# An expert stage with other weight rows, other sums and a fixed order on TensorE

## The chip, the core and the metric

The kernel runs on one core of one Trainium2 chip. Every time is in microseconds (us) of device time for one execution of the whole program. The core has a matrix engine (TensorE, in the profile PE for its products and PEld for its weight loads), a vector engine (VectorE, DVE), a scalar engine (ScalarE, ACT), GpSimd (POOL) and SyncE (SP), which here only issues DMAs. Each engine works through its own list of instructions in order and waits on semaphores for the others. Products are summed in eight PSUM banks of 128 partitions by 512 fp32 numbers.

## What is computed

Two transformer blocks over 256 tokens of width 1024. The first block (two layers, each with a feed-forward net, a token mix of four branches, a gated per-layer input and a second feed-forward net) and the mixer of the second block come first. The change is about what comes last, a mixture of experts: 32 experts, each token goes to four of them.

```python
def moe_ffn(h, w_router, b_router, w1, b1, w2, b2):
    logits = xt @ w_router + b_router
    top_v, top_e = lax.top_k(logits, TOP_K)          # 4 of 32
    weights = jax.nn.softmax(top_v, axis=-1)
    ...
    hcat = x_pad[tok] @ w1[e] + b1[e]                # [tokens, 1024] @ [1024, 2048]
    x_glu = jnp.minimum(hcat[:, ::2], SWIGLU_LIMIT)
    x_lin = jnp.clip(hcat[:, 1::2], -SWIGLU_LIMIT, SWIGLU_LIMIT)
    act = x_glu * jax.nn.sigmoid(SWIGLU_ALPHA * x_glu) * (x_lin + 1.0)
    return act @ w2[e] + b2[e]                       # [tokens, 1024] @ [1024, 1024]
```

The output is `x + g_f * moe_ffn(h, ...)`, where `h` is a modulated RMS norm of `x`. All weights are fp32.

## The kernel before, in words

**The first block and the mixer.** Their weights come through SP into 512 KB buffers named `raw`. ScalarE rounds each to float32r (`whi`, L143), VectorE or GpSimd subtracts (`wlo`, L147), and TensorE makes three products of each (L205 to L207). Layer norms run on VectorE (L266 to L275), token tile 0 first, then tile 1. Beside all this a side job `ada` multiplies the conditioning vector with a 1024 by 6144 matrix: 96 loads `araw` of 256 KB each on SP (L813), two buffers, and 96 sums `acc` on VectorE (L822). A list scheduler sets where those stand among the other instructions.

**The expert stage.** Experts go in 16 pairs, e and e+1, with room for 64 tokens each. For a pair, SP loads 24 weight units of 1 MB (L1440, tile `mraw`, and one buffer `AS`) into a ring of 18 buffers, in the order of their use: 16 for the up product, 8 for the down product. A unit is 256 rows by 1024 columns of one expert; row 128k+p lies on partition p, so each partition receives two runs of 4 KB. In the last pair the down units are 512 rows by 512 columns, in runs of 2 KB.

On TensorE one expert of the pair uses the left 64 columns of the array and the other the right 64. One up or down step is a product of 128x64 by 128x512 for each expert, and the two run side by side. The parts of a pair are: `moe_gather` (L1350, one-hot matrix `S` from L1338 times the tokens gives `xe`), `moe_bias` (L1379, a selector times the table `b1`, opens the banks), `moe_up` (L1389) for the first 1024 columns, then for the second, each followed by the activation (L1399 to L1403, with a tanh on ScalarE at L1400), `moe_aT` (L1409, transposes, copied by ScalarE at L1410), `moe_back` (L1363, the weighted return matrix `wT`), `moe_down` (L1423, scaled at L1427 into `ys`) and `combine` (L1471, `ys` times `wT`). `combine` adds the 16 pairs up in four banks over the whole stage; x is added at the very end (L1528) and stored (L1529). The gather and the bias of the next pair are given to the scheduler in the middle of the pair's second up product (`ahead`, L1512), so that their instructions stand among its steps.

Of the kernel before, what the change touches and what calls it, by code (L numbers as in the profile page):

```python
# [31 lines left out]
def constants():  # L32
    """Tables that depend on shapes alone."""
# [33 lines left out]
def arow(ap, n, parts=P):  # L67
    """A row of n numbers in DRAM, read by every partition."""
    return bass.AP(tensor=ap.tensor, offset=ap.offset, ap=[[0, parts], [1, n]])


class Kernel:
# [15 lines left out]
    # ---------------------------------------------------------------- helpers  # L88
# [31 lines left out]
    def rsqrt(self, v, eps, n, scale=1.0):  # L120
        """1/sqrt(v*scale+eps) by Newton steps on VectorE."""
# [19 lines left out]
    def split_from(self, src, hi, lo, pool=False):  # L141
        """hi = src rounded to float32r, lo = src - hi, both exact parts."""
# [36 lines left out]
    def gemms(self, lhs, nk, w, parts):  # L179
        """Several column ranges (first, width, done, onpool, granules) of one weight, tile 0 of all first."""  # L180
# [12 lines left out]
    def products(self, lhs, nk, width, banks, t, grans):  # L193
        """What the granules add to the banks of tile t."""
# [14 lines left out]
    def load_split(self, nk, w, c0, width, xn=0, onpool=()):  # L209
        """The granules of a weight: (first row chunk, number of chunks, hi, lo)."""  # L210
# [18 lines left out]
    def trans4(self, srcs, ident=None):  # L229
        """Up to four [128, <=128] pieces, transposed into one bank."""  # L230
# [5 lines left out]
    def to_T(self, src, t, xh, xl, c0, n):  # L236
        """chunks c0..c0+n of the natural tile src -> split, transposed tiles."""
# [12 lines left out]
    # --------------------------------------------------------------- layernorm  # L250
# [7 lines left out]
    def layer_norm(self, t, banks, coef, gb, last=False):  # L258
        """x[t] <- LN(coef*banks + x[t]); the new x^T; x[t] scaled for the next residual."""
# [33 lines left out]
    # -------------------------------------------------------------------- FFN  # L293
# [63 lines left out]
    def consts(self):  # L357
        """What comes beside the first product: the second tile of x, tables and constants."""
# [10 lines left out]
    def tables(self):  # L369
        """cos and sin of positions * inv_freq, [128, 2 tiles, 48]."""  # L370
# [34 lines left out]
    def gelu2(self, x, out, tmp):  # L405
        """out = 2*gelu(x) (tanh form)."""
# [7 lines left out]
    def proj(self, mp, lhs, w, c0, width, onpool=()):  # L414
        """natural [128, 2, width] of x @ w[:, c0:c0+width]."""
# [4 lines left out]
    def projs(self, mp, lhs, w, *parts):  # L420
        """Several of them, tile 0 of all first; a part is first column, width, onpool, granules."""
# [12 lines left out]
    def softmax_rows(self, S, n, keys, scale=1.0, extra=None):  # L434
        """In place exp(scale*(S - rowmax)) of S [128, n, keys]; returns 1/sum [128, n]."""
# [236 lines left out]
    def merge(self, mp, lhs, w_in, g0, wb, yTs, order, nk, then=None):  # L672
        """sum over n of 2*sigmoid(gate_n) * (y_n @ w_branch_n), natural [128, 1024] per tile."""
# [77 lines left out]
    def ple(self, L):  # L751
        """x[t] += sigmoid(x @ w_ple_gate) * (p @ w_ple); the second product fills the wait for the first."""
# [22 lines left out]
    # ----------------------------------------------------------- second block  # L775
# [14 lines left out]
    def ada(self, r0, r1):  # L790
        """Half rows r0.. of silu(c) @ w_ada + b_ada, into DRAM, in steps beside other work; 1 + both scales."""
# [42 lines left out]
    def mod_row(self, dst, i, norm=None):  # L834
        """dst [128, 1024] <- row i on every partition; with norm: row * norm."""
# [8 lines left out]
    def mod_pair(self, pool, i, norm):  # L844
        """The factor and the shift of a modulated norm."""
# [5 lines left out]
    def rms_mod(self, t, h, A, sh, split=True):  # L851
        """h <- x[t] * rsqrt(mean square) * A + sh, and its transpose, split or not."""
# [8 lines left out]
        xT = self.new_xT(t)  # L861
        for c in range(2):
            s = slice(c * 512, c * 512 + 512)
            nc.vector.scalar_tensor_tensor(h[:, s], x[:, s], r[:, 0:1], A[:, s], op0=OP.mult, op1=OP.mult)
            nc.vector.tensor_tensor(h[:, s], h[:, s], sh[:, s], op=OP.add)
# [8 lines left out]
    def lru_consts(self):  # L874
        """softplus(-lambda) times -2 and -4 per channel; half gate biases; conv weights."""
# [43 lines left out]
    def lru(self, mp, xr, gr, yT):  # L919
        """RG-LRU on [128 channels, 4, 256 tokens] tiles; writes its split output."""  # L920
# [25 lines left out]
        # with a = exp(L), u = tanh(L / 2): sqrt(1 - a^2) = sqrt(-u) * (1 + a)  # L946
# [22 lines left out]
    def rel_rows(self, mp):  # L969
        """Per head the bias row over query-key distance 255..-127, in DRAM; masked distances -1e30."""  # L970
# [13 lines left out]
        # one copy per partition, so that a pitch of one less skews the rows against each other  # L984
# [743 lines left out]
```

## Time and profile before

| what | value |
|---|---|
| time, median of 3 runs | 2582.32 us (2578.15 to 2583.32) |
| the profiled execution, span | 2582.4 us |
| TensorE busy | 2477.6 us, 96% of the span |
| VectorE, ScalarE, GpSimd busy | 1220.3, 815.1, 225.2 us |
| expert stage, first up step to the end | 1594 to 2582 us |
| share of 16 DMA engines in the expert stage | 102% (1700 to 2500 us) |
| HBM traffic | 704 MB read; 403 MB of it expert weights |

The profiled execution took as long as the median of the runs, so the sums of the prediction are made against its span. The span's first 60% belong to the first block and the mixer, the rest to the 16 pairs. The share of DMA time can pass 100% by a little, since transfers overlap at their edges. A matmul of fp32 leaves two records in the trace, so a step shows as two.

### The profile page before, as it was taken

To read this page: it belongs to the slowest core of one execution; us is meant where nothing else is said; L and a number is where in the kernel's file an instruction comes from. 1 tells how busy PE (TensorE), PEld (TensorE's weight loads), DVE (VectorE), ACT (ScalarE), POOL (GpSimd) and SP (SyncE) were. 2 spreads that over 40 slices of the span, in tenths; PEclk is the share of its full clock that TensorE was granted. 3 is DMA by queue.
4 is the path that set the end of the run, shared out by engine and by line. 5 is a ranking of instruction groups with operands and counts; after the bars stand their busy time and mean duration, and the time that the engine had idled before them with its cause. 6 is when DMAs were issued, how large, how long until landed. Compare 5 with 4: busy or idle time off the path is not lost.

```text
span 2582.4 us, 29195 instructions
## 1 busy us (share of the span) xinstructions
PE 2477.6 (96%) x11140; PEld 1611.5 (62%) x11140; DVE 1220.3 (47%) x2059; ACT 815.1 (32%) x1159; POOL 225.2 (9%) x197
## 2 busy tenths in 40 slices
PE   8999999999799999999988999999999999999998
PEld 6888787778678878778867776333333333333333
DVE  6767757776666775755567863111111111111111
ACT  5444544444344454444435641000000000000000
POOL 4000121200200011220031020000000000000000
PEclk9999999999899999999999998999999999999999
DMA  8775566667566646655655578999999999999995
GB/s 262 242 236 168 160 193 198 221 223 237 176 216 206 198 140 189 197 191 184 196 183 157 160 245 297 402 398 407 401 409 408 408 403 408 407 408 405 408 406 202
DMA packets 252697, 707.23 MB, mean 274 GB/s; under 512 B 18042, under 2 KB 31562, under 8 KB 252552
## 3 DMA queue, kind: packets, MB, share of 16 engines
q1 hardware_dynamic: 245032, 684.02, 73.9%
q0 software_dynamic: 7520, 21.29, 2.7%
q8 instruction: 90, 1.47, 0.2%
q14 instruction: 55, 0.45, 0.1%
HBM read 704.13 MB, written 3.47 MB: 274 GB/s over the span
## 4 chain that ended last, share of the span: by engine, by line
PE 77%; DVE 10%; DMA 5%; issue 4%; ACT 2%; POOL 1%; SPq 0%; DVEq 0%; ACTq 0%; POOLq 0%
PE sc L1389 19%; PE mm L206 12%; PE mm L207 12%; PE mm L205 12%; PE tp L1423 9%; PE tp L233 3%; PE tp L1350 2%; PE mm L1471 2%; DVE wlo L147 2%; DMA araw<-in_w_ada_dram 2%; PE sc L1379 1%; DMA raw<-in_ffn_up_dram 1%; ACT whi L143 1%; PE tp L1409 1%; DMA raw<-in_w_in_dram 1%
## 5 line engine op out<-in xcount | busy, mean ns | idle before, releaser
L147 DVE TENSOR_TENSOR wlo<-raw,whi 128x1024 fp32r<-128x1024 f32 (+1 forms) x459 | 568.8, 1246 | 292.4 <-ACT whi L143 289.9
L143 ACT ACTIVATE whi<-raw 128x1024 fp32r<-128x1024 f32 x486 | 509.6, 1055 | 538.2 <-PE mm L207 386.8
L206 PE MATMUL mm<-wlo,xTh 128*128 128x512 f32 (+2 forms) x1552 | 593.8, 383 | 9.5 <-POOL wlo L147 8.3
L205 PE MATMUL mm<-whi,xTh 128*128 128x512 f32 (+2 forms) x1552 | 599.6, 387 | 3.4 <-ACT whi L143 3.4
L207 PE MATMUL mm<-whi,xTl 128*128 128x512 f32 (+2 forms) x1552 | 594.0, 383 | 0.4 <-DVE xTl L147 0.4
L1389 PE MATMUL sc<-mraw,xe 128*64 128x512 f32 x1904 | 494.8, 598 | 0.0
L206 PEld LDWEIGHTS mm<-wlo,xTh 128*128 128x128 f32 x1552 | 295.4, 190 | 67.8 <-POOL wlo L147 11.3
L205 PEld LDWEIGHTS mm<-whi,xTh 128*128 128x128 f32 x1552 | 295.5, 191 | 61.0 <-ACT whi L143 5.9
L207 PEld LDWEIGHTS mm<-whi,xTl 128*128 128x128 f32 x1552 | 295.5, 190 | 52.4 <-DVE xTl L147 0.8
L1389 PEld LDWEIGHTS sc<-mraw,xe 128*64 128x64 f32 x1904 | 166.7, 136 | 254.0 <-issue 247.1
L1400 ACT ACTIVATE mt<-act 128x256 f32<-128x256 f32 x64 | 26.7, 417 | 720.8 <-DVE act L1399 708.6
L1423 PE MATMUL tp<-mraw,xTl 128*64 128x512 f32 x936 | 235.2, 595 | 9.8 <-ACT xTl L1410 9.6
L1399 DVE TENSOR_SCALAR act<-sc 128x256 f32<-128x256 f32 x62 | 26.3, 424 | 362.7 <-PE sc L1389 359.5
L1423 PEld LDWEIGHTS tp<-mraw,xTl 128*64 128x64 f32 x936 | 72.9, 137 | 148.7 <-issue 135.0
L1427 DVE TENSOR_TENSOR xTh<-tp,gf 128x512 f32<-128x512 f32 x32 | 22.1, 691 | 245.6 <-PE tp L1423 245.6
L207 PE MATMUL mm<-whi,hl 128*128 128x512 f32 x352 | 138.0, 392 | 0.0
L205 PE MATMUL mm<-whi,hh 128*128 128x512 f32 x352 | 137.8, 391 | 0.0
L206 PE MATMUL mm<-wlo,hh 128*128 128x512 f32 x352 | 137.6, 391 | 0.0
L822 DVE SCALAR_TENSOR_TENSOR acc<-araw,cond,acc 128x512 f32<-128x512 f32 x96 | 75.7, 788 | 50.2 <-DMA araw<-in_w_ada_dram 49.6
L147 POOL TENSOR_TENSOR wlo<-raw,whi 128x1024 fp32r<-128x1024 f32 x27 | 69.6, 2593 | 280.9 <-ACT whi L143 277.0
L694 POOL TENSOR_TENSOR pj<-pj,gt 128x512 f32<-128x512 f32 x32 | 58.1, 1827 | 239.3 <-DVE gt L693 238.1
L206 PEld LDWEIGHTS mm<-wlo,hh 128*128 128x128 f32 x352 | 66.4, 189 | 13.4
(423 smaller groups left out, 2178.4 us busy)
## 6 DMA issues: line engine op xcount, KB each, us to landing
mraw<-in_w_dram SPq DMA_DIRECT2D x362, 1024.0 KB, 16.2
raw<-in_ffn_up_dram SPq DMA_DIRECT2D x176, 512.0 KB, 4.4
raw<-in_w_in_dram SPq DMA_DIRECT2D x142, 512.0 KB, 4.2
raw<-in_ffn_down_dram SPq DMA_DIRECT2D x88, 512.0 KB, 4.3
araw<-in_w_ada_dram SPq DMA_DIRECT2D x96, 256.0 KB, 3.8
AS<-in_w_dram SPq DMA_DIRECT2D x21, 1024.0 KB, 14.8
raw<-in_w_branch_dram SPq DMA_DIRECT2D x28, 512.0 KB, 3.8
raw<-in_w_out_dram SPq DMA_DIRECT2D x24, 512.0 KB, 4.6
```

What stands on the lines that cost most here:

```text
L143: ins = self.nc.scalar.activation(hi, src, AF.Copy)
L147: ins = (self.nc.gpsimd if pool else self.nc.vector).tensor_tensor(lo, src, hi, op=OP.subtract)
L205: nc.tensor.matmul(banks[b], xh, hi[:, s], start=kc == 0, stop=False)
L206: nc.tensor.matmul(banks[b], xh, lo[:, s], start=False, stop=False)
L207: nc.tensor.matmul(banks[b], xl, hi[:, s], start=False, stop=kc == nk - 1)
L233: self.nc.tensor.transpose(pt[:s.shape[-1], i * P:i * P + s.shape[0]], s, self.ident)
L694: nc.gpsimd.tensor_tensor(m, m, th, op=OP.add)
L822: nc.vector.scalar_tensor_tensor(acc, raw, self.cond[:, k:k + 1], acc, op0=OP.mult, op1=OP.add)
L1350: nc.tensor.matmul(pg[c // 4][:, c % 4 * P:c % 4 * P + P], self.h2[t][:, c * P:c * P + P], S[:, t], start=t == 0 and c % 4 == 0, stop=t == ...
L1389: self.upped = nc.tensor.matmul(ph[nb][e * 64:e * 64 + 64], xe[:, k, e * 64:e * 64 + 64], u[:, (k % 2) * D + nb * 512:(k % 2) * D + nb * 5 ...
L1423: nc.tensor.matmul(py[c][e * 64:e * 64 + 64], aT[:, k * P + e * 64:k * P + e * 64 + 64], u[:, :512], start=k == 0, stop=k == 7)
L1471: self.nc.tensor.matmul(out[t][c], w[:, t, :], ys[:, c * 512:c * 512 + 512], start=start, stop=stop)
```

## The change

- **Weight rows.** Row 8p+k lies on partition p. A unit is one such k for the up product (2048 columns) or two for the down product (2 times 1024 columns): each partition receives one run of 8 KB. From partition to partition the addresses step by 64 KB in the up weights and by 32 KB in the down weights. The last pair's down product loads its first four k like the others and the last four by column halves, in runs of 2 KB. What meets the weights is permuted to match: `rms_mod` reads x and its two factors at a step of eight numbers for the expert norm (L864, L865 of before), the router's rows are loaded as 8p+k, and the last operation of the activation writes in another order.
- **The up product** runs over all 2048 columns at once in four banks: for k below 6 all four banks for each k, then k = 6 and 7 bank by bank. The activation follows for four banks.
- **Sums into x.** Every pair's `combine` goes into banks of its own and VectorE adds the result to x, one pair later.
- **Biases** are multiplied in float32r: the table is split into a high and a low part in 128 rows, two tables for 32 experts, so a selector of 512 columns and four products remain.
- **TensorE in program order.** All products of the stage pass through `pe`, which forbids the scheduler to move them.
- The DMA scratch of the program is set to 8192 bytes, which also moves where tiles lie.

```diff
     def route_prep(self, mp):
-        nc.gpsimd.dma_start(wr, a["w_router_2"][0].rearrange("(k p) n -> p k n", p=P))
+        nc.gpsimd.dma_start(wr, a["w_router_2"][0].rearrange("(p k) n -> p k n", k=KD))
...
+        for i in range(2):
+            raw = self.st(self.wp, [P, 1024], "raw", bufs=self.nraw)[:, :512]
+            hl = self.st(mp, [P, 512], f"b1{i}", F32R)
+            for h in range(2):
+                nc.gpsimd.dma_start(raw[64 * h:64 * h + 64], src[64 * i:64 * i + 64])
+            self.pin(nc.scalar.activation(hl, raw, AF.Copy))
+            self.pin(nc.vector.tensor_tensor(hl[64:], raw[64:], hl[64:], op=OP.subtract))
...
+    def pe(self, ins):
+
+        self.pin(ins)
+        return ins
...
     def moe_up(self, mp, xe, ph, units):
...
+        cut = KD - 2
+        steps = [(k, nb) for k in range(cut) for nb in range(4)] + [(k, nb) for nb in range(4) for k in range(cut, KD)]
+        for k, nb in steps:
+            for e in range(2):
+                self.pe(nc.tensor.matmul(ph[nb][e * 64:e * 64 + 64], xe[:, k, e * 64:e * 64 + 64],
+                                         units[e][k][:, nb * 512:nb * 512 + 512], start=False, stop=k == KD - 1))
...
-            nc.vector.scalar_tensor_tensor(g, l, 1.0, g, op0=OP.add, op1=OP.mult)
+            o = act.rearrange("s (k p) -> s p k", k=KD)[:, 32 * nb:32 * nb + 32]
+            nc.vector.scalar_tensor_tensor(o, l.rearrange("s (p k) -> s p k", k=KD), 1.0,
+                                           g.rearrange("s (p k) -> s p k", k=KD), op0=OP.add, op1=OP.mult)
...
     def sources(self, e):
-                return w[e + d, r, c].rearrange("(k p) n -> p k n", p=P)
-            return w[bass.ds(e[d], 1), r, c].rearrange("o (k p) n -> p (o k) n", p=P)
-        up = [rows(W1, d, j, q * D) for q in range(2) for j in range(4) for d in range(2)]
...
+                v = w[e + d].rearrange("(p k) n -> p (k n)", k=KD)
+            else:
+                v = w[bass.ds(e[d], 1)].rearrange("o (p k) n -> p (o k n)", k=KD)
+            return v[:, j * n:j * n + n]
+        up = [rows(W1, d, j, 2 * D) for j in range(8) for d in range(2)]
...
+    def combine(self, ys, w, cs=(0, 1), out=False):
+        for c in cs:
+            s = slice(c * 512, c * 512 + 512)
             for t in range(2):
-                self.nc.tensor.matmul(out[t][c], w[:, t, :], ys[:, c * 512:c * 512 + 512], start=start, stop=stop)
+                po = self.ps("tp")
+                self.pe(nc.tensor.matmul(po, w[:, t, :], ys[:, s], start=True, stop=True))
+                nc.vector.tensor_tensor(self.x[t][:, s], self.x[t][:, s], po, op=OP.add)
...
     def moe(self, mp):
         for e in range(0, NE, 2):
...
+            act = self.moe_up(mp, xe, ph, u1)
+            if end:
+                self.combine(*done)
+            else:
+                xe = self.moe_gather(mp, self.pos[:, :, e + 2:e + 4])
+            wT = self.moe_back(mp, self.pos[:, :, e:e + 2], self.Wh[:, :, e:e + 2])
+            self.moe_aT(act, aT)
+            self.moe_down(aT, ys, u2, (lambda: self.combine(ys, wT, (0,), True)) if end else None)
...
+            if done:
+                self.combine(*done)
...
+            done = ys, wT
+            ph = bias(e + 2)
...
-    nc = _bacc.Bacc("TRN2", target_bir_lowering=False, num_devices=1)
+    nc = _bacc.Bacc("TRN2", target_bir_lowering=False, num_devices=1, dynamic_dma_scratch_size=8192)
```

TensorE before, in the second half of a pair's up product: the rows L1389 are up steps of this pair, L1350 the gather of the next one, L1363 the return matrix.

```order
L1389 MATMUL sc_16242<-mraw_16162,xe_16077 64x512
L1363 MATMUL tp_16302<-ident,Sw_16298 128x128
L1350 MATMUL tp_16317<-S_16313,h_13106 128x128 x4
L1350 MATMUL tp_16318<-S_16313,h_13106 128x128 x2
L1389 MATMUL sc_16241<-mraw_16164,xe_16077 64x512
L1389 MATMUL sc_16242<-mraw_16164,xe_16077 64x512
L1350 MATMUL tp_16318<-S_16313,h_13106 128x128 x2
L1350 MATMUL tp_16317<-S_16313,h_13107 128x128 x4
L1389 MATMUL sc_16241<-mraw_16166,xe_16077 64x512
L1389 MATMUL sc_16242<-mraw_16166,xe_16077 64x512
```

TensorE now, at the end of a pair's up product (L1417 its last steps, L1369 the gather of the next pair, L1382 the return matrix, L1439 the transposes of the activation, L1456 the first down step).

```order
L1417 MATMUL mm_16768<-mraw_16801,xe_16671 64x512
L1417 MATMUL mm_16768<-mraw_16803,xe_16671 64x512
L1369 MATMUL sc_16922<-S_16918,h_13118 128x128 x4
L1369 MATMUL sc_16923<-S_16918,h_13118 128x128 x4
L1369 MATMUL sc_16922<-S_16918,h_13119 128x128 x4
L1369 MATMUL sc_16923<-S_16918,h_13119 128x128 x4
L1382 MATMUL tp_16946<-ident,Sw_16942 128x128 x2
L1439 MATMUL tp_16952<-ident,act_16885 128x128 x4
L1439 MATMUL tp_16958<-ident,act_16885 128x128 x4
L1456 MATMUL sc_16965<-mraw_16805,xTl_3743_16951 64x512
```

The gather stood between up steps, and up steps of one expert came two in a row; now it stands in one piece behind the last step, and the steps of the two experts alternate.

VectorE before, in the layer norm that closes the first feed-forward net of layer 0 (x_71 is token tile 0, mm the banks).

```order
L266 SCALAR_TENSOR_TENSOR x_71<-mm_1527,x_71 128x512
L267 BN_STATS bn_353_1747<-x_71 128x6
L266 SCALAR_TENSOR_TENSOR x_71<-mm_1528,x_71 128x512
L267 BN_STATS bn_353_1747<-x_71 128x6
L269 BN_AGGR mv_354_1752<-bn_353_1747 128x2
```

VectorE now, at the same place.

```order
L266 SCALAR_TENSOR_TENSOR x_71<-mm_1527,x_71 128x512
L267 BN_STATS bn_353_1747<-x_71 128x6
L822 SCALAR_TENSOR_TENSOR acc_4070<-araw_4073,cond,acc_4070 128x512
L822 SCALAR_TENSOR_TENSOR acc_4070<-araw_4075,cond,acc_4070 128x512
L266 SCALAR_TENSOR_TENSOR x_71<-mm_1528,x_71 128x512
L822 SCALAR_TENSOR_TENSOR acc_4070<-araw_4090,cond,acc_4070 128x512
L267 BN_STATS bn_353_1747<-x_71 128x6
L822 SCALAR_TENSOR_TENSOR acc_4070<-araw_4099,cond,acc_4070 128x512
L269 BN_AGGR mv_354_1752<-bn_353_1747 128x2
```

Sixteen sums of the side job, which stood in the second feed-forward net of layer 0, now stand in this layer norm and the start of the token mix behind it.

SP at the same place, the difference of the two lists (raw_1942 and its neighbours are weights of the token mix).

```order
 L219 DMA raw_1942<-in_w_in_dram 128x2x512
+L808 DMA acc_4070<-in_b_ada_dram 1x512
+L813 DMA araw_4073<-in_w_ada_dram 128x512
+L813 DMA araw_4075<-in_w_ada_dram 128x512
+L808 DMA acc_4267<-in_b_ada_dram 1x512
+L813 DMA araw_4090<-in_w_ada_dram 128x512
+L813 DMA araw_4099<-in_w_ada_dram 128x512
+L813 DMA araw_4116<-in_w_ada_dram 128x512
+L813 DMA araw_4125<-in_w_ada_dram 128x512
 L219 DMA raw_1948<-in_w_in_dram 128x2x512
```

The loads of the side job stand ahead of weight loads of the token mix; with two buffers `araw`, each waits until VectorE has used the one before the last.

## Rows read from the trace of the kernel before

**Rows 1.** The head of the page.
```profile
span 2582.4 us, 29195 instructions
```
**Rows 2.** Busy time by stretch; the last three: granted clock, DMA share, GB/s.
```profile
1595.00:1600.00 5.00, 5.00 (x26) 1.57 (x24) 0.00 (x0) 0.00 (x0) 0.00 (x0) 1.00 0.19 33
...
1700.00:2500.00 800.00, 785.08 (x3239) 304.19 (x3236) 121.93 (x309) 53.20 (x116) 0.00 (x0) 1.00 1.02 406
2056.00:2058.00 2.00, 2.00 (x12) 1.17 (x12) 0.15 (x1) 0.00 (x0) 0.00 (x0) 1.00 1.03 410
...
2540.00:2542.00 2.00, 2.00 (x10) 0.74 (x7) 0.00 (x0) 0.00 (x0) 0.00 (x0) 1.00 1.05 390
...
2546.00:2549.00 3.00, 3.00 (x16) 1.26 (x14) 0.00 (x0) 0.00 (x0) 0.00 (x0) 1.00 0.73 274
```
**Rows 3.** Waits of SP's queue, 1620 to 2582: total us, times, longest.
```profile
SPq L1440 <- PE sc L1389: 377.3, 136, 9.4
SPq L1440 <- PE tp L1423: 207.0, 100, 9.6
```
**Rows 4.** The chain that ended last, one pair: start us, us, what.
```profile
1698.37 13.95 PE tp L1423 x62
1712.32 3.63 PE mm L1471 x8
1715.95 13.95 PE sc L1389 x64
...
1729.93 0.42 DVE act L1399
...
1731.20 0.44 PE tp L1409 x2
...
1739.01 1.34 PE tp L1350 x12
...
1759.60 0.61 ACT xTl L1410
...
1760.25 4.93 PE tp L1423 x21
```
**Rows 5.** Groups by line and shape, 1700 to 2500 (13 pairs): count, busy, mean ns.
```profile
L1379 PE MATMUL sc<-b,sel 128*128 128x512 f32 x102 | 56.7, 637 | 2.1
```
**Rows 6.** The chain at the start of the expert stage.
```profile
1590.42 3.57 PE mm L1350 x16
1593.99 11.36 PE mm L1389 x49
```
**Rows 7.** Adding the shift in the expert norm, L865: ns min/median/max.
```profile
L865 DVE TENSOR_TENSOR h<-h,AS x4: 681/682/683, 1568.0 to 1581.5; 128x512 f32<-128x512 f32 x4
```
**Rows 8.** The chain at the end of the stage.
```profile
2574.70 2.00 PE mm L1471 x4
...
2576.73 0.69 DVE xTl L1528
```
**Rows 9.** Stretches at half clock, columns as in rows 2.
```profile
1588.10:1594.90 6.80, 6.52 (x28) 5.55 (x30) 3.08 (x19) 1.19 (x2) 0.00 (x0) 0.50 1.02 405
...
656.30:666.50 10.20, 3.05 (x12) 2.71 (x13) 8.64 (x23) 1.25 (x3) 0.00 (x0) 0.50 0.56 177
...
536.80:540.20 3.40, 3.40 (x12) 2.65 (x11) 3.30 (x6) 0.60 (x1) 0.00 (x0) 0.50 0.54 177
```
**Rows 10.** The chain in two layer norms, at 200 us and at 645 us.
```profile
200.28 0.70 DVE x L266
...
209.76 0.63 PE tp L233 x4
...
646.91 5.58 DMA araw<-in_w_ada_dram
...
663.45 1.08 PE tp L233 x4
...
667.12 0.23 PE mm L205
```

More of the change, by code (lines that the diff above doesn't have):

```diff
@@ new lines, in moe_up, with moe_aT @@
+            nc.vector.scalar_tensor_tensor(o, l.rearrange("s (p k) -> s p k", k=KD), 1.0,
+                                           g.rearrange("s (p k) -> s p k", k=KD), op0=OP.add, op1=OP.mult)
+        return act
+    def moe_aT(self, act, aT):
+        for q in range(2):
+            pt = self.ps("tp")
+            for j in range(4):
+                c = slice((q * 4 + j) * P, (q * 4 + j) * P + P)
+                self.pe(self.nc.tensor.transpose(pt[:, j * P:j * P + P], act[:, c], self.ident))
+            self.nc.scalar.activation(aT[:, q * 512:q * 512 + 512], pt, AF.Copy)
@@ new lines, in moe_down, with step, scale @@
+    def moe_down(self, aT, ys, units, last=None):
+        nc = self.nc
+        py = [self.ps("sc") for _ in range(2)]
+        def step(k, c):
+            for e in range(2):
+                if last and k >= 4:
+                    w = units[e][2 + c][:, k % 4 * 512:k % 4 * 512 + 512]
+                else:
+                    w = units[e][k // 2][:, k % 2 * D + c * 512:k % 2 * D + c * 512 + 512]
+                self.pe(nc.tensor.matmul(py[c][e * 64:e * 64 + 64], aT[:, k * P + e * 64:k * P + e * 64 + 64], w,
+                                         start=k == 0, stop=k == 7))
+        def scale(c):
+            s = slice(c * 512, c * 512 + 512)
+            nc.vector.tensor_tensor(ys[:, s], py[c], self.gf[:, s], op=OP.mult)
@@ L1417, in moe_down @@
         steps = [(k, c) for k in range(KD) for c in range(2)]
         if last:
-            steps.sort(key=lambda kc: kc[1])
+            steps = steps[:8] + [(k, c) for c in range(2) for k in range(4, KD)]
         for k, c in steps:
-            for e in range(2):
-                u = units[e][2 * c + k // 4][:, k % 4 * 512:] if last else units[e][k // 2][:, k % 2 * D + c * 512:]
-                nc.tensor.matmul(py[c][e * 64:e * 64 + 64], aT[:, k * P + e * 64:k * P + e * 64 + 64], u[:, :512],
-                                 start=k == 0, stop=k == 7)
@@ L1425, in moe_down @@
-        for c in range(2):
-            s = slice(c * 512, c * 512 + 512)
-            nc.vector.tensor_tensor(ys[:, s], py[c], self.gf[:, s], op=OP.mult)
+            step(k, c)
+            if k == 7:
+                scale(c)
+            if last and (k, c) == (5, 1):
+                last()
     def mtile(self):
@@ L1519, in moe @@
-            acc = acc or [[self.ps("mm") for c in range(2)] for t in range(2)]
-            self.combine(ys, wT, acc, e == 0, e == NE - 2)
-            if e == 0:
-                self.bias2(mp, acc)
-                nov = nc.values_load(self.nov[0:1, 0:1], min_val=0, max_val=NOV - 1)
-        self.acc = [self.big(f"xT{h}0") for h in "hl"]
-        for c in range(2):
-            for t in range(2):
-                s = slice(c * 512, c * 512 + 512)
-                nc.vector.tensor_tensor(self.acc[t][:, s], self.x[t][:, s], acc[t][c], op=OP.add)
-                nc.sync.dma_start(self.out[0, t * P:t * P + P, s], self.acc[t][:, s])
+            end = e == NE - 2
@@ new lines, in moe @@
+            act = self.moe_up(mp, xe, ph, u1)
+            if end:
+                self.combine(*done)
+            else:
+                xe = self.moe_gather(mp, self.pos[:, :, e + 2:e + 4])
+            wT = self.moe_back(mp, self.pos[:, :, e:e + 2], self.Wh[:, :, e:e + 2])
+            aT = self.big(f"xTl{i}")
+            self.moe_aT(act, aT)
+            ys = self.big(f"xTh{i}")
+            self.moe_down(aT, ys, u2, (lambda: self.combine(ys, wT, (0,), True)) if end else None)
+            if end:
+                self.combine(ys, wT, (1,), True)
+                break
@@ L1538, in bias2 @@
         for t in range(2):
-            nc.tensor.transpose(pw[:NE, t * P:t * P + P], self.W[:, t], self.ident)
-        wT = self.st(mp, [P, 2, P], "wT")[:NE]
+            self.pe(nc.tensor.transpose(pw[:NE, t * P:t * P + P], self.W[:, t], self.ident))
+        wT = self.st(mp, [P, 2, P], "wT", bufs=2)[:NE]
         nc.scalar.activation(wT, pw[:NE, :256].rearrange("p (t q) -> p t q", t=2), AF.Copy)
-        for t in range(2):
-            for c in range(2):
-                nc.tensor.matmul(acc[t][c], wT[:, t, :], b2[:, c * 512:c * 512 + 512], start=False, stop=False)
+        self.combine(b2, wT)
     def overflow(self, mp, nov):
```

151 lines of the change are left out of this document (63 added, 88 removed).

## The prediction

> **What bounds the kernel now.** I read the table of stretches first. From 1700 to 2500 us TensorE is busy 785 of 800 us at full clock, and in the same stretch the DMA engines run at a share of 1.02 and move 406 GB/s [rows 2]. Both are full, so the next question is who waits for whom. The waits of SP's queue answer it: the weight loads wait 377.3 and 207.0 us for up and down steps to free a buffer [rows 3]. TensorE sets the pace and the DMA follows close behind. The chain of one pair gives the pace: the down products of two pairs start at 1698.37 and 1760.25, so a pair takes 61.9 us [rows 4]. A pair's weights are 24 x 1.0486 = 25.2 MB, which at 406 GB/s is 62.0 us and at the 410 of an undisturbed stretch 61.4 us [rows 2]. A change that only shortens TensorE's pair can therefore win next to nothing; one that only speeds up the loads neither. This one touches both, and the sum must be made for each.
>
> The start and the end tell how much of the DMA's time lies between. In 1595 to 1600 it moves 33 GB/s, because the ring is full until the first up steps have run, and the rate falls again in 2546 to 2549 [rows 2]. The 366 units after the first 18 are 383.8 MB; at 406 GB/s they take 945 us, and 1600 + 945 = 2545, which agrees. The remaining 37 us to the end of the span at 2582.4 [rows 1] are TensorE working off its backlog.
>
> **The loads, 8 KB runs.** Before has only 4 KB runs, and 2 KB runs in the last pair. With 16 engines, 390 GB/s at 2 KB is 32768/390 = 84.0 ns a run; 406 to 410 at 4 KB is 161.4 to 159.8 ns [rows 2]. Another 2 KB thus costs 77.4 to 75.8 ns and the fixed part is 7 to 8 ns. By the same line a run of 8 KB takes 316 to 311 ns, or 414 to 421 GB/s. I take 417: 383.8/0.417 = 920 us, 25 us less. No row shows 8 KB runs, so the bounds are wide: above, no fixed part at all, 131072/(4 x 75.8) = 432 GB/s and 888 us; below, the 390 GB/s of the slowest runs shown and 984 us. I stay near the line through the two rows, since they are the same queue, the same tensors and the same ring.
>
> The Trainium skill, "DMA: Bandwidth & Descriptors", section "Latency and other measured facts", speaks against the new addresses: copies whose partitions lie a large power of two apart ran at 207 GB/s for a step of 512 KB and 103 for 4 MB, against 214 otherwise. Here the step is 64 and 32 KB, smaller than any in that list, and no row of before shows such a step. By a loss of the first size (207/214) 417 would become 403 GB/s and the gain would be gone; it is the second rival below.
>
> **TensorE's pair.** Up: two halves of 13.95, 27.9 us. Down 13.95, combine 3.63 [rows 4]. The gather: 12 records take 1.34, so its 32 take 3.6; ten transposes as long as such a record 1.1 [rows 4]. The biases were 102 records and 56.7 us in 13 pairs, 4.4 a pair [rows 5]; four float32r products at 0.23 [rows 10] are 0.9. Idle: after the last up step the activation of the last bank must run (1729.93 to 1731.20, 1.3 us [rows 4]) and the one-hot matrix of the gather is queued behind it on VectorE, an estimated 1 us more; the copy of the transposes, 0.6 [rows 4]; the selector behind the sums into x, about 1.2 by one sum as long as the last addition [rows 8] and its own copy. Sum 55.2 us. What it saves against 61.9 lies in the second up product: the 28.4 us from 1731.20 to 1759.60 [rows 4] hold 13.95 of up steps beside transposes, gather, biases and the idle time of the activation, and steps of one expert in a row, which lose the overlap of the two experts. What the program order costs is cover: gather and transposes now have no up steps beside them. The clock may follow. The shortest stretch at half clock (0.50 of the full 2.4 GHz) that the rows show lasts 3.4 us, at 536.8 [rows 9], and costs half of that. With two of them, 1.7 us each, a pair is 58.6.
>
> A pair's loads at 417 GB/s are 60.4 us. So the loads bind, TensorE catches up in a few pairs, and then waits 2 to 5 us a pair, at the last two k of the up product. Four sums of 0.69 into x per pair and the strided write of the activation lie on VectorE, which has 122 us of work in 800 [rows 2]: free.
>
> **The start.** The whole gather of pair 0 now stands behind all routing. Half of it was done earlier; the half that was left took 3.57 us at half clock [rows 6, 9], so the up product starts 3.6 us later than 1593.99. The strided reads of the norm are not shown in before. The operations are 0.68 us each [rows 7] and four per tile lie on the path: between nothing and twice as long, 0 to 2.8 us. I take 1, since most of the path around them is TensorE's. The loads resume at 1600 + 4.6 = 1604.6.
>
> **The end.** Loads end at 1604.6 + 920.4, plus 0.7 for four units in 2 KB runs: 2525.7. The last up unit lands 8 units, 20.8 us, before that. From it: 7 of the 32 up steps 6.1, activation 1.3, the waiting combine 3.6, transposes 1.1, copy 0.6, down 13.95 with half a combine 1.8 inside, 28.5 us, which is 7.7 behind the last load. Then scale 0.7, combine 2.0 and addition 0.7 [rows 8], and the store: the last addition ended at 2577.4 and the span at 2582.4, 5.0. That is 16.1, where before had 37. End: 2541.8.
>
> **Layer 0.** The lists show a term that the edit does not name: 16 sums of the side job and their loads move from the second feed-forward net into the layer norm at 200 us. That norm takes 9.5 us before TensorE gets its transposes [rows 10]. The norm at 645 has sums between its instructions in the very order that the first one now gets; from its wait for the load (5.58 us) to the transposes it takes 16.5 us, 7 more, and TensorE comes out of it with 10.2 us at half clock, 5 more [rows 9, 10]. Token tile 1 follows with sums too, and weight loads of the token mix queue behind the side job's. So up to 20 us can be lost. Gains stand against this: the second feed-forward net loses those sums, its half-clock stretch at 537 among the possible savings [rows 9]. Bounds -4 and +20; I take +8, nearer the norm at 645 than nothing. Forecast 2541.8 + 8 = 2550.
>
> **Rivals.**
> 1. The loads get no faster with longer runs. Then 945 instead of 920 us and 2575. For it: 410 GB/s may be the limit of something else than runs. Against: 390 and 410 differ with the run alone.
> 2. The loads get slower: every partition's run lies 64 KB from the next, and what serves the addresses takes that badly. It decides from 403 GB/s on (953 us to the end at 2582); at 390, 2613. For it only the page; against it no row, since before has steps of 4 and 8 KB.
> 3. TensorE's order binds. If every idle moment costs a half-clock stretch as long as the 6.8 us of the routing [rows 9], a pair is 55.2 + 6.8 = 62.0. Then 1598.6 + 15 x 62.0 + 58.7 for the last pair and its end + 8 = 2595, slower. It decides from 61.1 a pair. For it: three idle moments per pair where before had covered ones. Against: the idle moments are shorter than those in the norms.
> 4. All of it works and layer 0 costs nothing: 421 GB/s and 2533, with the gain of 4 there 2529.
>
> **Chances.** Forecast (2535 to 2570) 0.57, rival 1 0.13, rival 2 0.10, rival 3 0.08, rival 4 0.12. A measurement of this kernel can tell about 0.2% from no change. Faster: 0.56 of the forecast, all of rival 4, 0.06 of rival 1: 0.74. Same: 0.01, 0.06 of rival 1 and 0.03 of rival 3: 0.10. Slower: rival 2, 0.05 of rival 3 and 0.01 of rival 1: 0.16. The range from 2520 to 2592 leaves out the worse half of rivals 2 and 3 and a rate above 428 GB/s.
>
> **What would show it.** Right: 415 to 420 GB/s between 1700 and 2500, SP's queue no longer waiting for up and down steps but up steps for loads, a pair of 60 us, and some 17 us between the last load and the end. The layer norm at 200 us shows sums and a gap of several us on TensorE. Wrong: a rate at or under 406 (rivals 1 and 2), or half clock in each pair with SP still waiting for TensorE (rival 3).

## The result, and the profile after

The changed kernel takes 2553.7 us, the median of four runs (2552.11 to 2555.68), against 2582.82 for the kernel before: a ratio of 0.990 (95%: 0.9883 to 0.9916), faster by about 1%. Its profiled execution has a span of 2550.5 us, where before had 2582.4 [rows 1]. All readings of after in this section are of that execution.

The head of the page of after, and the shares of the span on its chain of waits by engine:

```profile
span 2550.5 us, 29146 instructions
...
PE 40%; DMA 36%; DVE 7%; issue 2%; ACT 2%; POOL 1%; SPq 0%; DVEq 0%; ACTq 0%; POOLq 0%
```

DMA is 36% of the chain: over a third of the span ends on a transfer. The loads of expert weights, the tiles `mraw` and `AS`, are 31 of these 36 points.

Stretches of after (length, busy time of PE, PEld, DVE, ACT, POOL; then granted clock, DMA share, GB/s): the layer norm at 210, a gap in the mixer, the start of the expert stage with the ring still full, the bulk of the stage, and its last up steps.

```profile
209.60:216.50 6.90, 0.00 (x0) 0.00 (x0) 6.90 (x15) 0.00 (x0) 0.00 (x0) 0.67 0.94 271
...
1519.20:1526.00 6.80, 3.38 (x7) 2.27 (x8) 3.17 (x3) 3.69 (x4) 0.00 (x0) 0.50 0.92 327
...
1610.00:1615.00 5.00, 5.00 (x26) 1.68 (x24) 0.00 (x0) 0.00 (x0) 0.00 (x0) 1.00 0.21 51
1615.00:1620.00 5.00, 5.00 (x26) 1.61 (x24) 0.00 (x0) 0.00 (x0) 0.00 (x0) 1.00 1.00 418
...
1700.00:2450.00 750.00, 695.77 (x3118) 266.37 (x3114) 161.16 (x343) 50.69 (x108) 0.00 (x0) 0.98 1.01 421
...
2510.00:2516.00 6.00, 5.18 (x13) 1.49 (x14) 1.78 (x4) 0.42 (x1) 0.00 (x0) 0.51 1.01 415
```

The bulk row answers to the 406 GB/s of [rows 2]: the DMA share is still full, the rate is 421, and TensorE now has 54 us of idle time in 750 where it had 15 in 800.

Waits of SP's queue in after, 1620 to 2550 (total us, times, longest):

```profile
SPq L1482 <- DMA mraw<-in_w_dram: 654.2, 315, 3.1
SPq L1482 <- PE mm L1417: 41.4, 42, 7.6
SPq L1482 <- PE sc L1456: 17.2, 16, 7.1
```

The 377.3 and 207.0 us for TensorE [rows 3] have become 41.4 and 17.2. What a load waits for now is an earlier load.

The chain of after: one pair at the start, when the ring still has weights in stock, and one late in the stage.

```profile
1609.33 27.62 PE mm L1417 x128
1636.95 3.78 PE sc L1369 x32
...
1641.68 0.66 PE tp L1439 x4
1642.34 13.88 PE sc L1456 x64
1656.54 0.94 PE mm L1404 x4
...
1658.48 3.81 PE tp L1526 x8
...
2431.68 19.83 DMA mraw<-in_w_dram
2451.56 7.64 PE mm L1417 x26
2459.20 3.78 PE sc L1369 x32
...
2464.58 6.88 PE sc L1456 x31
2471.47 19.78 DMA mraw<-in_w_dram
```

Early, the whole chain is TensorE: up 27.6, gather 3.8, down 13.9, biases 0.9, combine 3.8. Late, the chain goes through the landing of a unit before every stretch of matmuls. Between 1700 and 2450 TensorE waits for units in 41 short pieces:

```profile
PE mm L1417 <- DMA mraw<-in_w_dram: 44.3, 37, 1.4
PE mm L1417 <- DMA AS<-in_w_dram: 6.3, 4, 2.4
```

Their 50.6 us in 750, which hold 12.5 pairs of loads at 59.8 us (25.17 MB at 421 GB/s), are 4.0 us a pair. So the limit has moved from TensorE to the loads, and the loads run 15 GB/s faster.

### The profile page after: what moved, and what is told of

Read it like the earlier page. It is cut to its first block, busy times and chain, and to the rows that moved or that the text cites. A ratio compares the mean times of both kernels' runs of the same rounds, so it can differ in the third digit from the quotient of the medians.

```text
span 2550.5 us, 29146 instructions
## 1 busy us (share of the span) xinstructions
PE 2385.5 (94%) x11076; PEld 1571.2 (62%) x11076; DVE 1279.3 (50%) x2126; ACT 817.6 (32%) x1161; POOL 227.1 (9%) x200
## 4 chain that ended last, share of the span: by engine, by line
PE 40%; DMA 36%; DVE 7%; issue 2%; ACT 2%; POOL 1%; SPq 0%; DVEq 0%; ACTq 0%; POOLq 0%
DMA mraw<-in_w_dram 28%; PE mm L206 10%; PE mm L207 10%; PE mm L205 10%; DMA AS<-in_w_dram 3%; PE mm L1417 3%; PE tp L233 2%; DVE wlo L147 2%; DMA raw<-in_w_in_dram 1%; PE sc L1456 1%; DMA araw<-in_w_ada_dram 1%; ACT whi L143 1%; POOL wlo L147 1%; PE sc L1369 1%; DVE x L274 0%
## 5 line engine op out<-in xcount | busy, mean ns | idle before, releaser
L1417 PE MATMUL mm<-mraw,xe 128*64 128x512 f32 x1968 | 495.4, 615 | 49.3 <-DMA mraw<-in_w_dram 49.3
L1417 PEld LDWEIGHTS mm<-mraw,xe 128*64 128x64 f32 x1968 | 156.3, 141 | 367.2 <-issue 265.5
L1426 ACT ACTIVATE mt<-mg 128x256 f32<-128x256 f32 x64 | 26.7, 417 | 812.4 <-DVE mg L1425 762.4
L1425 DVE TENSOR_SCALAR mg<-mm 128x256 f32<-128x256 f32 x64 | 27.2, 425 | 462.1 <-PE mm L1417 457.7
L1456 PE MATMUL sc<-mraw,xTl 128*64 128x512 f32 x936 | 223.4, 594 | 0.2 <-ACT xTl L1440 0.2
L1456 PEld LDWEIGHTS sc<-mraw,xTl 128*64 128x64 f32 x936 | 71.5, 137 | 140.2 <-issue 136.7
L1461 DVE TENSOR_TENSOR xTh<-sc,gf 128x512 f32<-128x512 f32 x32 | 22.1, 692 | 215.7 <-PE sc L1456 215.7
```

Of the source, the lines that this page charges most:

```text
L1417: self.pe(nc.tensor.matmul(ph[nb][e * 64:e * 64 + 64], xe[:, k, e * 64:e * 64 + 64], units[e][k][:, nb * 512:nb * 512 + 512], start=False, ...
L1425: nc.vector.tensor_scalar(g, pv[:, :, 0], 7.0, None, op0=OP.min)
L1426: nc.scalar.activation(th, g, AF.Tanh, scale=0.851)
L1456: self.pe(nc.tensor.matmul(py[c][e * 64:e * 64 + 64], aT[:, k * P + e * 64:k * P + e * 64 + 64], w, start=k == 0, stop=k == 7))
```

## The experiments

Each run's theories are quoted as they were written before it. Ratios are against the kernel before, run on the same chip; by that measure after has 0.990. They ran on four chips, on which the kernel before took 2579.4 to 2583.3 us, so the times of two changed kernels can differ by some us from the chip alone.

**Run length: 4 KB.** The new order and addresses, each 8 KB row fetched by two DMAs.

```diff
-            self.nc.sync.dma_start(r, src)
+            for h in range(2):
+                self.nc.sync.dma_start(r[:, h * D:h * D + D], src[:, h * D:h * D + D])
```

> Every 8 KB unit row is fetched by two DMAs of 4 KB per partition; addresses, order and products stay. Theory (a run costs a fixed part plus its bytes): the rate in the stage falls from 421 to 406-410 GB/s, 383.8 MB take 936 to 945 instead of 912 us, the time is 2577 to 2587. Rival (the rate came with the new addresses or with whole-unit rows, not with the length of the runs): 421 GB/s and 2554 within 3.

2581.46 us, 1.0007 (0.9993 to 1.0021). Its bulk row:

```profile
1700.00:2450.00 750.00, 683.79 (x3038) 263.19 (x3036) 161.09 (x343) 50.68 (x108) 0.00 (x0) 0.97 1.03 409
```

The rate falls back to the 406 to 410 of before, and the whole gain is gone, although TensorE's order is the new one. SP's queue still waits for loads (503.4 us), so the loads bind at 4 KB too.

**Run length: 2 KB.** The same with four pieces.

```diff
-            self.nc.sync.dma_start(r, src)
+            for h in range(4):
+                self.nc.sync.dma_start(r[:, h * 512:h * 512 + 512], src[:, h * 512:h * 512 + 512])
```

> Every 8 KB unit row is fetched by four DMAs of 2 KB per partition. Theory (a run costs a fixed part plus its bytes; 8 KB ran at 421, 4 KB at 409): about 390 GB/s in the stage, 383.8 MB take 984 us, the time is 2620 to 2630. Rival (two or more DMAs per unit cost by their number, not by the run): each further DMA costs what the second did, 25 us, so four give 2554 + 3 x 25 = 2630 too, but the rate of the shares, 1.02 to 1.06 of the engines busy, would not rise.

2633.09 us, 3 us above the range of the theory, in one run, at 385 GB/s where 390 had been expected:

```profile
1700.00:2450.00 750.00, 657.82 (x2856) 245.92 (x2854) 148.05 (x315) 46.46 (x99) 0.00 (x0) 0.96 1.05 385
```

With 16 engines, 385, 409 and 421 GB/s are 85.1, 160.2 and 311.3 ns a run. The first 2 KB more cost 75.1, the next 4 KB 151.1, twice 75.6. The line that the prediction drew through two rows holds at the third length, with a fixed part of 9 to 10 ns where it had 7 to 8. In these two runs the number of DMAs grows as the runs get shorter, which was the rival. The kernel before tells the two apart: it fetched each unit with one DMA, in runs of 4 KB, at 406 to 410 GB/s [rows 2], as the two DMAs a unit do here at 409. The length of the runs counts, not the number of DMAs.

**Address step.** The up units take rows 128k+p, so partitions step by 8 KB instead of 64; the down units keep their step of 32 KB. The matching order of the activations is left out, so the products meet other rows; the work is the same.

```diff
-        up = [rows(W1, d, j, 2 * D) for j in range(8) for d in range(2)]
+        def flat(d, j):
+            if isinstance(e, int):
+                return W1[e + d, j * P:j * P + P, :]
+            return rows(W1, d, j, 2 * D)
+
+        up = [flat(d, j) for j in range(8) for d in range(2)]
```

> The up weights come as rows 128k+p, so that each 1 MB unit is one contiguous block: 8 KB runs stay, the step from partition to partition is 8 KB instead of 64 KB. The products then meet the wrong rows of the activations; the work is the same. Theory (only the run counts): 421 GB/s and 2554 within 3. Rival (a large step between partitions costs rate): the rate rises above 425 GB/s, and with 2/3 of the bytes faster the time falls by 6 us or more.

2550.95 us, 0.9878 (0.9852 to 0.9904), and again 421 GB/s:

```profile
1700.00:2450.00 750.00, 693.87 (x3122) 266.31 (x3116) 161.10 (x343) 50.67 (x108) 0.00 (x0) 0.98 1.01 421
```

The rate doesn't change: a step of 64 KB costs nothing against one of 8 KB. The time is within the noise of after's (0.9878 against 0.990, with overlapping intervals).

**What TensorE has in hand.** The combine's matmul written twice.

> The changed kernel with every combine product made twice into the same bank: 3.6 us more of TensorE's work in each of 16 pairs. Theory (the loads bind and TensorE waits about 4 to 5 us a pair for the last units): the pair stays near 60 us, only the last pair's share at the end shows, 2 to 5 us: 2555 to 2559. Rival (TensorE's order binds): 15 x 3.6 = 54 us more, about 2608.

2559.49 us, 0.9919 (0.9904 to 0.9934), half a us above the range of the theory:

```profile
1700.00:2450.00 750.00, 725.95 (x3275) 287.96 (x3274) 165.83 (x356) 54.06 (x115) 0.00 (x0) 0.99 1.01 421
```

Still 421 GB/s, while TensorE's busy time rose from 695.77 to 725.95. Only 5.8 us reach the end, where sixteen pairs with 3.6 us more each would show over 50 if TensorE bound. The loads bind.

**The program order undone.**

```diff
     def pe(self, ins):
-        self.pin(ins)
```

> The changed kernel without program order on TensorE: the scheduler may place gather, biases and transposes among the up steps again. Theory (the loads bind, the order has slack): 2552 to 2558. Rival (the fixed order is what made the pair short; with woven products TensorE's pair is 61.9 us as before): 15 x 2 = 30 us more, about 2584.

2718.03 us, 1.0533 (1.0512 to 1.0554). Neither number was met: a pair takes 70 us. Waits of SP's queue in this kernel, 1700 to 2600:

```profile
SPq L1481 <- PE sc L1455: 398.0, 77, 15.9
SPq L1481 <- PE mm L1416: 374.9, 202, 5.6
```

Loads wait for TensorE again, and the rate is 360 GB/s. TensorE itself waits 61.8 us in the bulk with a bias product at the head of its queue. Two more runs ask which part of the order does it.

**Only the biases in order**, all else free.

```diff
-    def pe(self, ins):
-        self.pin(ins)
+    def pe(self, ins, bias=False):
+        if bias:
+            self.pin(ins)
...
-            self.pe(self.nc.tensor.matmul(ph[nb], sel[:, nb], b1, start=True, stop=False))
+            self.pe(self.nc.tensor.matmul(ph[nb], sel[:, nb], b1, start=True, stop=False), True)
```

> As e7_free_order, but the four bias products stay behind what was written before them. Theory (in e7 the next pair's biases stood ahead of the transposes and TensorE waited there for the activation to empty the four banks, 9 us a pair, at 70 us a pair): the pair falls to 60 to 63 us and the time to 2555 to 2600. Rival (what cost e7 its time is the woven gather and combine): 2680 or more.

2734.42 us, 1.0581 (1.0559 to 1.0602): the theory that the bias products are to blame falls. Waits of TensorE in this kernel, 1700 to 2450:

```profile
PE tp L1440 <- DVE act L1431: 93.0, 11, 8.5
```

Left to itself the up product ends in all four banks together, so the whole activation stands between it and the transposes: 8.5 us a pair.

**Up steps and biases in order**, gather, down and combine free.

> As e10_bias_in_order, but the up steps keep their written order too; gather, return matrix, transposes, down product and combine stay free, and the gather stands early among the up steps. Theory (what costs e7 and e10 their 10 us a pair is the order of the up steps: experts no longer in turn, and all four banks ending together, so that TensorE idles for the whole activation of four banks): the idle time after the up product falls from 8.5 to 2 to 3 us, up takes 28 to 29 us, the loads bind again and the time is 2550 to 2562. Rival (the woven gather, or the down product and combine out of order, cost it): 2640 or more.

2607.14 us, 1.0109 (1.0092 to 1.0126), still slower than before; neither number was met. The wait for the activation falls to 40.9 us in 12, 3.4 each. The chain of one pair in this kernel, and the start of its down product as a stretch:

```profile
1957.20 10.26 PE sc L1457 x36
1967.46 1.91 PE tp L1527 x4
1969.38 3.58 PE sc L1457 x12
1972.96 1.91 PE tp L1527 x4
1974.87 1.86 PE sc L1457 x4
1976.73 0.90 PE mm L1405 x3
1977.63 3.58 PE sc L1457 x12
1981.20 0.44 PE mm L1405
...
1957.20:1960.10 2.90, 2.90 (x8) 0.99 (x10) 0.00 (x0) 0.44 (x1) 0.00 (x0) 0.50 1.01 421
```

Down, combine and biases take 24.4 us from 1957.20 to 1981.64; in order they take 13.88 + 0.94 + 3.81 = 18.6. Part of these 5.8 us is the clock: TensorE stands idle for the activation just before, and the down product then begins at half clock (0.50), in this pair as in each of the others. In after the gather fills that place. The first 36 down records take 10.26 us, 2.5 more than 36 of after's (0.217 us each). The other 28 run at full clock, and still take 9.0 us where 28 of after's take 6.1: this is the order of the steps alone.

Against the 70 us a pair of the two runs above, the order of the up steps is worth about 8 us a pair, of which 5 are the shorter wait for the activation (against the run before). What is left against after is the 5.8 us here and the 3.4 of uncovered activation. With both, a pair takes 62.1 us. That is longer than its loads (59.8 us), and SP's queue waits for TensorE again (345.5 and 323.8 us between 1700 and 2500).

**Layer 0: the scratch setting alone**, in the kernel before.

```diff
-    nc = _bacc.Bacc("TRN2", target_bir_lowering=False, num_devices=1)
+    nc = _bacc.Bacc("TRN2", target_bir_lowering=False, num_devices=1, dynamic_dma_scratch_size=8192)
```

> The kernel before with nothing but the DMA scratch of 8192 bytes. Theory (the scratch alone frees the room that lets the side job's loads start early): the 16 sums stand in the layer norm at 200 us, TensorE has a gap of about 7 us there, and since moving them away took 8 us off the changed kernel, the time is 6 to 9 us above before. Rival (the expert stage's new code moves them): the lists and the time of before, within 2 us.

2586.28 us, 1.0022 (1.0013 to 1.0031), a little less than the 6 to 9 us of the theory. In its profiled execution, which took 5 us longer than the median, the up product starts at 1600.9 instead of 1594.0. TensorE's wait in this kernel, 195 to 230:

```profile
PE tp L233 <- DVE x L275: 6.1, 1, 6.1
```

The 16 sums stand at the norm here too (from 200.8 us on; before has none between 195 and 260). The side job's move comes from this one argument and costs some 5 us.

**Layer 0: the side job's loads held back** in after, behind the latest layer weight.

```diff
...
-                nc.sync.dma_start(raw, self.wsrc(w, j % KD, 1, j // KD * 512, 512)[:, 0, :])
+                with tc.issue_after(self.lastraw.ins) if r0 == 4 else nullcontext():
+                    nc.sync.dma_start(raw, self.wsrc(w, j % KD, 1, j // KD * 512, 512)[:, 0, :])
```

> The loads of the side job's second part are queued behind the weight that is next at that place, so its 16 sums leave the layer norm at 200 us and go back into the second feed-forward net of layer 0. Theory (the changed kernel is 6.8 us late at the end of that norm and 3 to 4 us late at 663): the gap of 7 us at 209 goes, half of it comes back in the feed-forward net, the time falls by 3 to 4 us to 2550. Rival (the norm's loss is whole and nothing comes back): the time falls by 7 or more.

2545.05 us, 0.9849 (0.9823 to 0.9874). The gap at 210 is gone, and 8.7 us with it (by the ratios more), which is what the rival had said: the loss is not given back on the way.

**The first expert units behind the last gate weights** in after.

```diff
+            if i == 5 and late:
+                late()
...
-            self.nc.sync.dma_start(r, src)
+            ins = self.nc.sync.dma_start(r, src)
+            if hold:
+                self.pin(ins)
```

> The first four expert units stand again behind the mixer's gate weights on SP's queue, as before the change. Theory (four 1 MB loads ahead of a gate weight cost 10 us of waiting there, TensorE idle for 6.9 us and then at half clock): the gap at 1515 goes, the up product starts 8 to 11 us earlier, the time is 2543 to 2547. Rival (what is loaded early is not loaded later, and the DMA idles at 1605 to 1615 anyway): 2552 to 2555.

2552.18 us, 0.9873 (0.9844 to 0.9903). The theory failed; the time is the rival's. The gap of 6.9 us that the next section shows is gone, but the mixer now waits 4.3 us for GpSimd at 1553.6, with a stretch at half clock behind it:

```profile
1555.60:1562.40 6.80, 4.53 (x16) 3.85 (x17) 4.36 (x6) 3.69 (x5) 3.41 (x2) 0.50 0.92 317
```

The up product starts at 1611.4, no earlier than the 1609.3 of after. A wait for GpSimd at this place isn't new: before has one of 2.9 us, after one of 1.1.

**Both, and the side job's third part later too** (its loads behind the weights, and eight steps later).

```diff
+                with tc.issue_after(self.lastraw.ins) if r0 else nullcontext():
...
+            for _ in range(8 if r0 == 8 else 0):
+                yield
```

> The changed kernel with the first expert units behind the gate weights, and with the side job's second and third part queued behind the weights at their place, the third 8 weights later, so that no layer norm of layer 0 holds such sums. Theory: 8 us of the norm at 200 as when moved alone, and the norm at 650 loses its two gaps of 8 and 6 us and 2 x 3.4 to 5 us at half clock, of which half may come back later: 2530 to 2536. Rival (the loads and sums cost the same wherever they stand): 2543 to 2546.

2535.47 us, 0.9814 (0.98 to 0.9827): the best version, 18 us below after by the times and more by the ratios. The same without the third part:

> The first expert units behind the gate weights and the side job's second part behind its weights, without the third part's move that e8 has. Theory (the early units cost nothing by themselves, as e3 showed; the third part's move gives the 10 us between e4 and e8): 2543 to 2547. Rival (the units' order matters once the norm's loss is gone): 2536 to 2540.

(the edits of the last two single runs together): 2544.02 us, 0.985 (0.9832 to 0.9868), the time of the side job's loads held back alone. So the units' place adds nothing, and the third part's move brings the other 8.5 us.

## Why the prediction was right

It named 2550 us, and the kernel takes 2553.7. The mechanism is the one it described: faster loads and a shorter pair on TensorE, the loads binding, TensorE waiting some us a pair. The sizes of the loads, the start and the end were off and nearly cancel; that the sum came within 4 us is in this part luck.

**The loads.** 421 GB/s against 417, so 383.8 MB take 912 us instead of 920. From the ring's restart at about 1615 to the last up unit at 2511.2 passed 896 us; the prediction had 900 (1612.6 to 2512.9, with its 8 us of layer 0). Rival 1 (no faster) is dead by the runs of 2, 4 and 8 KB. Rival 2 (the step) is dead for 64 KB by the run with 8 KB steps. The 32 KB of the down units were not changed by themselves. The rule of the Trainium skill ("DMA: Bandwidth & Descriptors", section "Latency and other measured facts") that the prediction weighed begins with a step of 512 KB. It does not reach down to the 64 KB of this kernel, and no run here has a step as large as those it lists.

**TensorE's pair.** With next to no waits it is 51.6 to 54.7 us (transposes of the activation at 1641.68, 1696.33, 1747.96, 1801.80; 1.1 us of waiting for a load in the last of the three), predicted 55.2. The longest of them has a stretch at half clock. The term too many was the idle time after the up product, 1.3 for the activation and 1 for the one-hot matrix. The gather starts at 1636.95, the moment the up product ends, and covers the activation; the one-hot matrix has been made earlier. Of the 61.9 us before, 3.5 went with the biases (4.4 us a pair then [rows 5], 0.94 now); no run brought the old biases or the old sums back by themselves.

Rival 3 did not come. From the first pair on until TensorE waits for loads there is one stretch at half clock, of 3.4 us at 1662.6; the others, from 1908 on, stand beside such waits and show in no rate. But the rival's mechanism is real, and the runs that undo the order show how near it was. With up steps and biases alone in order each pair has a stretch of 3 to 8 us at half clock, in the two runs with less order one of 7 to 11; the mean granted clock from 1700 to 2450 is 0.97 there and 0.94 and 0.93 here. At 62.1 us a pair, where the rival had 62.0, the kernel is slower than before. That the program order saves time was argued from the second up product; against the scheduler's own order of the new code the runs put it at about 8 us a pair for the up steps and some 8 to 10 for what follows (62.1 against 51.6 to 54.7), half clock included.

**The sum of the two.** With 4 KB runs and the new order: no gain. With 8 KB runs and the free order: 5% slower. The gain belongs to the pair of edits, as the prediction's first paragraph had it. That long runs alone would win next to nothing in the old kernel is argued from its pair of 61.9 us and not shown: no run has them with the old order.

**The start.** The up product starts 15.3 us later, predicted 3.6 + 1 + 8 = 12.6, but the time is lost in other places than predicted. Three moments of the chain, in us: the 0.66 us step of the mixer's VectorE work (L1135 of before, L1143 of after), the first addition of the mixer's result into x (L1254, L1262), and the first up step.

| kernel | mixer step | first addition | first up step |
|---|---|---|---|
| before | 1450.9 | 1562.3 (111.4 later) | 1594.0 (31.7 later) |
| before, scratch setting | 1455.9 | 1569.6 (113.7) | 1600.9 (31.4) |
| after | 1453.9 | 1573.7 (119.8) | 1609.3 (35.6) |
| side job held back | 1446.9 | 1569.1 (122.2) | 1605.2 (36.1) |
| units behind gates | 1455.9 | 1573.9 (118.0) | 1611.4 (37.4) |
| best version | 1442.2 | 1560.1 (117.9) | 1597.7 (37.6) |

The rows of before and after, on which the sizes below rest; the last is the gather of after.

```profile
1450.90 0.66 DVE s L1135
1562.31 0.70 DVE y L1254
...
1453.90 0.66 DVE s L1143
1573.73 0.70 DVE y L1262
...
1603.50 5.83 PE sc L1369 x32
```

Each row of the table is one execution. Three more runs (4 KB, the 8 KB step and the combine twice) have the code of after up to the expert stage, but for the way in which the first two fetch their units, and give 1452.2 to 1453.5, 122.2 to 123.5 and 35.9 to 36.5. With the combine twice the mixer takes 122.3 against 119.8 by the same instructions, so differences of 2 or 3 us in the table show nothing by themselves.

Gather and norm cost 3.9, predicted 4.6. The gather of 32 products took 5.83 us (3.78 in the pairs behind, at full clock), and the strided reads made an operation of the norm over half as long again (after, L873; before in [rows 7]):

```profile
L873 DVE TENSOR_TENSOR h<-h,AS x4: 1067/1082/1132, 1580.2 to 1594.4; 128x512 f32<-128x512 f32 x4
```

The Trainium skill ("SBUF — State Buffer", section "Door 1: The DMA port swizzle") says that fp32 reads with a step of more than four numbers pay a penalty; the trace agrees for a step of eight, with 1.08 against 0.68 us.

Layer 0 costs 3.0 at the mixer's step (1.3 to 3.0 with the three more runs), predicted 8. The mechanism is there: waits of after, 198 to 218, of the side job's sums for their loads and of the transposes behind them.

```profile
DVE acc L822 <- DMA araw<-in_w_ada_dram: 7.4, 2, 6.0
...
PE tp L233 <- DVE x L275: 7.0, 1, 7.0
```

Of these 7 us 3.0 are left at the mixer's step in after, but 5.0 in before with the scratch setting, and holding the loads back wins 7.0 there, which makes it faster than before. The term was real, and its size seems to depend on what else in layer 0 ends last, which no run shows; 8 was too much for after.

What the prediction missed is 8.4 us inside the mixer (up to 12 in the three more runs). The four expert units that are loaded ahead now stand eight weight loads earlier on SP's queue than before, in front of the last six gate weights, and a gate weight lands late:

```profile
1507.14 14.26 DMA raw<-in_w_in_dram
...
1521.47 1.06 ACT whi L143
```

TensorE idles 6.9 us for it, and runs at half clock around it (0.50 from 1519.2 to 1526.0). Yet the run with the units moved back did not win these microseconds: its mixer takes 118.0, its routing 1.8 longer than after, and its time is that of after. The late weight is thus one of several things that end last; the wait for GpSimd may be the next. The scratch setting alone lengthens the mixer by 2.3, which is within this spread. Which part of the new code brings the 8 to 12 us stays open; the preparation of the bias table on VectorE and ScalarE lies in this stretch, but no run took it away.

**The end.** From the last up unit to the last down step 31.2 us, predicted 28.5. The chain of after, and the last up steps of TensorE's list:

```profile
2491.31 19.84 DMA mraw<-in_w_dram
2511.19 5.12 PE mm L1417 x11
2516.33 0.44 DVE mg L1425
...
2522.02 2.06 PE tp L1526 x4
...
2543.08 2.00 PE tp L1526 x4
2545.10 0.69 DVE x L1527
...
2511.19 8.54 PE L1417 MATMUL mm<-mraw,xe 128*64 128x512 f32 x26 [0.82 <-DMA mraw<-in_w_dram]
```

The up steps that wait for the last unit take 8.5 us where the prediction had 6.1. TensorE has waited for each of the last units, and it runs them at half clock (0.51 from 2510 to 2516, in the rows of the first section). This is nearly all of the 2.7 us. From the last up step, at 2519.7, to the transposes, at 2524.9, pass 5.2 us, where the prediction had 1.3 for the activation and 3.6 for the waiting combine. The parts differ: the chain runs through the activation from 2516.33 to 2521.97, because the last steps of the banks come close together when the last unit has only just landed, and three banks of activation queue on VectorE and ScalarE. But the combine runs beside the last of them. Scale, combine and store were as predicted: from the last down step to the end 8.2 us, predicted 8.4.

Against the predicted 2549.8, the start is 2.4 us later at the ring's restart, the loads 4.1 shorter and the end 2.4 longer. That makes the profiled 2550.5.

**Rival 4.** Layer 0 free and 421 GB/s were to give 2533. The best version, which is free of this loss and of some that before had, takes 2535.5. From its first up step (1597.7) to its end (2537.0) pass 939 us, against 941 in after. With these loads the length of the expert stage stays the same in both, and the gain lies in its start.

## What to carry to other kernels

Where two limits lie within a per cent of each other, work out both and change both; taking either the long runs or the order out of the new kernel took the whole gain away here. Mind the clock when you set the order: without it each pair had an idle moment and a stretch at half clock. Draw the cost of a DMA run as a line through two rows of different length and extend it, and when a stage that waits for loads ends, price its last steps at the clock that they get: half clock was hidden in the middle and cost 2.4 us at the end. Compare the two instruction lists over the whole program, since a setting of memory size moved a side job, and loads issued ahead moved past weights, in stages that the edit does not name.

## What the runs showed of the hardware

- A run of 2, 4 or 8 KB takes 85, 160 or 311 ns on one of the 16 engines: 9 to 10 ns fixed and 75 ns for each 2 KB, with no flattening up to 421 GB/s on this core. The number of DMAs that a unit is split into doesn't show: 4 KB runs gave 406 to 410 GB/s with one DMA of 1 MB and 409 with two of 512 KB.
- Runs 64 KB apart from partition to partition are fetched as fast as runs 8 KB apart (421 GB/s both).
- Half clock on TensorE (0.50 granted, 1.2 of 2.4 GHz) shows in no rate where loads bind: after has a mean of 0.98 in its bulk, and doubling the combine raised it to 0.99, both at 421 GB/s. It shows where TensorE sets the time: the last up steps of after took 8.5 us where 6.1 had been predicted.
- VectorE's addition of 128x512 fp32 numbers took 1.08 us with one operand at a step of eight numbers and 0.68 with all of them contiguous.
